# The high part of every fourth weight unit by a casting DMA, in a two-layer encoder trunk on one core

## The chip, the cores and the metric

One core of one Trainium2 chip runs the whole forward pass in one launch. The metric is the device time of that launch in microseconds (us); lower is better. The reference is in float32, and the kernel keeps to its accuracy by splitting every operand of a large product in two.

## The reference

Two post-norm layers over 256 tokens of 2048 channels. The first mixes tokens with bidirectional gated linear attention, the second with a 2-D neighbourhood attention of 16 heads; each is followed by a gated conv feed-forward with 5632 channels in either half. Cut to what matters here:

```python
for i in range(DEPTH):                      # DEPTH = 2
    m = _gla_mixer(x, ...) if i % 2 == 0 else _na_mixer(x, ...)
    x = _layer_norm(DEEPNORM_ALPHA * x + m, ln_mix_g[i], ln_mix_b[i])
    f = _conv_ffn(x, ffn_w_up[i], ffn_conv_w[i], ffn_conv_b[i], ffn_w_down[i])
    x = _layer_norm(DEEPNORM_ALPHA * x + f, ln_ffn_g[i], ln_ffn_b[i])

def _conv_ffn(x, w_up, conv_w, conv_b, w_down):
    h = x @ w_up
    hp = jnp.pad(h, ((0, 0), (1, 1), (0, 0)))
    h = hp[:, :-2] * conv_w[0] + hp[:, 1:-1] * conv_w[1] + hp[:, 2:] * conv_w[2] + conv_b
    a, b = jnp.split(h, 2, axis=-1)
    return (jax.nn.gelu(a, approximate=False) * b) @ w_down
```

In the neighbourhood attention a head computes `softmax(q k * scale + bias)` over its window and multiplies by v.

## The kernel before

All weights are cut into 393 units in the order in which TensorE takes them (`unit_plan`); all but one are of 1 MB, 128 partitions of 2048 float32. A "ws" unit holds 128 output channels for all 2048 input channels and stands still in the array while the tokens stream; an "as" unit holds 512 input channels by 512 output channels and is streamed against the activations.

TensorE multiplies float32r, a rounded float32. So a unit is loaded into a `raw` buffer (three of them, by SyncE's DMA queue, L127) and split: `hi` is the rounded copy, made by ScalarE (L131), and `lo` the rest, made by VectorE (L132), each in four pieces of 512 columns. There are four `hi` and four `lo` buffers (`NS = 4`), so that a unit's `hi` goes into the buffer that TensorE read four units earlier. A product takes three terms: hi by hi, hi by lo and lo by hi (L190).

`pump` writes the splits and loads into the program: when a unit has been used (`finish`), the split of the unit four later is emitted, with a priority lowered by `SPLIT_AFTER = 20`. A tile framework then sets each engine's order by the priorities and adds the waits. Each engine works strictly in that order.

Beside the split VectorE evacuates the products. In the feed-forward's up-projection it joins two halves (L461), waits for GpSimd's multiply of the convolution (L642), adds two taps (L643, L644) and multiplies the gate (L660). In attention it joins q and k, scales and biases the scores into `s` (L724), takes the maximum (L728), and after ScalarE's exponential the reciprocal (L733), and scales `s` (L735), which TensorE then transposes (L742). A head's scores, transposes and last product are put into TensorE's order between the products of the following weights, a fixed number of steps after its k (`later(score, 3, ...)`, `turn` 7, `pv` 9). GpSimd also issues the loads of biases (L701) and LayerNorm parameters (L344).

```python
    def emit_split(src, hi, lo):
        nc.scalar.copy(hi, src)
        nc.vector.tensor_tensor(lo, src, hi.bitcast(F32), ALU.subtract)
```

Of the kernel before, what the change touches and what calls it, by code (L numbers as in the profile page):

```python
# [10 lines left out]
F32 = mybir.dt.float32  # L11
# [6 lines left out]
P = 128  # L18
# [29 lines left out]
def unit_plan():  # L48
    """The 1 MB weight units in the order in which the tensor engine takes them."""
    plan = []  # L50
    for h in range(HG):
        plan += [("ws", "gla_in", h * 2 + c) for c in range(2)]
        plan += [("ws", "gla_in", 8 + h * 2 + c) for c in range(2)]
        if h == 0:
            plan += [("lr",)]
        plan += [("as", "gla_in", 4 + h, u) for u in range(4)]
        plan += [("as", "gla_in", 8 + h, u) for u in range(4)]
    plan += [("as", "gla_out", nb, u) for nb in range(4) for u in range(4)]
    for layer in range(DEPTH):
        if layer == 1:  # L60
            for g in range(4):
                plan += [("as", "na_in", 8 + g, u) for u in range(4)]
                for h in range(4 * g, 4 * g + 4):
                    plan += [("ws", "na_in", h), ("ws", "na_in", 16 + h)]
            plan += [("as", "na_out", nb, u) for nb in range(4) for u in range(4)]
        for c0, n in THIRDS:
            if c0 == 0:
                plan += [("pairs", f"up{layer}", u) for u in range(4)]
            for c in range(c0 + (2 if c0 == 0 else 0), c0 + n):
                plan += [("ws", f"up{layer}", c), ("ws", f"up{layer}", NCT + c)]  # L70
            plan += [("as", f"down{layer}", nb, u)
                     for nb in range(4) for u in range(c0 // 4, (c0 + n) // 4)]
    return plan
# [3 lines left out]
def kernel(  # L77
# [36 lines left out]

    raws, splits = {}, {}
    st = {"load": 0, "split": 0, "done": 0, "next": 0, "tick": 0}

    def pieces(n):
        return [slice(c * 2048 // n, (c + 1) * 2048 // n) for c in range(n)]

    def emit_load(j):
# [12 lines left out]
    def pump():  # L134
        while st["split"] < min(n_units, st["done"] + NS):
# [4 lines left out]
            r = raws.pop(j)  # L140
            hi = hi_p.tile([P, 2048], F32R, tag="hi", name="hi")
            lo = lo_p.tile([P, 2048], F32R, tag="lo", name="lo")
            if plan[j][0] == "lr":
                # three copies of the columns, for the three terms of the gates' product
                src = r[:, :512].rearrange("p (k m) -> p k m", m=32)
                h4 = hi[:, :KC * 96].rearrange("p (k c m) -> p k c m", c=3, m=32)
                l4 = lo[:, :KC * 96].rearrange("p (k c m) -> p k c m", c=3, m=32)
                for c in range(3):
                    emit_split(src, h4[:, :, c], l4[:, :, c])
            else:  # L150
                for sl in pieces(4):
                    with tc.high_priority(offset=-SPLIT_AFTER):
                        emit_split(r[:, sl], hi[:, sl], lo[:, sl])
            splits[j] = (hi, lo)
            st["split"] = j + 1
            if st["load"] < n_units:
# [3 lines left out]
    def take():  # L160
        """The parts of the next unit."""
        pump()
# [10 lines left out]
    def later(fn, delay=1, chain=True):  # L173
        """Emit fn in `delay` ticks: after the item queued before it, or from now on."""
        now = st["tick"]
# [15 lines left out]

# [1 line left out]
    def ws_part(xs, hi, lo, ps, kcs):  # L193
# [15 lines left out]

# [1 line left out]
    def as_mm(xs, k, kc, hi3, lo3, ps, t, start, stop):  # L211
# [4 lines left out]
    def as_block(xs, n, evac, apart=False, settle=False):  # L216
        """n units (4 chunks of K each) for one block of 512 columns."""
        ps = [ps_mm(), ps_mm()]
# [41 lines left out]

# [1 line left out]
    ident = const.tile([P, P], F32, name="ident")  # L262
# [6 lines left out]

# [1 line left out]
    def rsqrt(dst, src, scale, eps, small):  # L271
        """(src * scale + eps) ** -0.5"""
        m = small.tile([P, 1], F32, tag="rs_m", name="rs_m", bufs=2)
# [13 lines left out]
    def ln_mid(pool, xs, t, stats, idx, gb):  # L287
        """LayerNorm between sub-layers: xT for the products, xs for the residual."""
        def head():
# [57 lines left out]
    def residual_out(act_in, first, last, n, idx, begin=None):  # L347
        """Four blocks of columns of a product that ends a sub-layer, and the LayerNorm after it."""
        stats = {}
# [23 lines left out]

# [1 line left out]
    scope = {"stack": ExitStack()}  # L375
# [15 lines left out]

    # the first units and x in pieces of K, so that the products start with the first of them
    n_first = NR
# [32 lines left out]

    # the gates as one product over 98 rows: (lr, weights) as (hi, hi), (lo, hi), (hi, lo), and the bias
    lrT = gla.tile([98, T], F32R, name="lrT")
    nc.gpsimd.memset(lrT[96:98, :].bitcast(F32), 1.0)
    # +1 on the rows with weights' high parts, -1 on those with their low parts; 0 and 1  # L430
    sgn = gla.tile([98, 2], F32, name="sgn")
# [24 lines left out]
    def join(pool, dst, ps):  # L456
        """The sum of the two parts of a weights-stationary product."""
        ps4 = ps.rearrange("p (t h n) -> p t h n", t=2, h=2)
# [4 lines left out]
    def gla_head(h):  # L463
# [17 lines left out]
        def gates(z):  # L481
# [12 lines left out]
            else:  # L494
                nc.vector.tensor_tensor_scan(c_[:, ::-1], smask[:, 512:0:-1], la[:, ::-1], 0.0, ALU.mult, ALU.add)
            # [channel, tile of channels, block of 128, half, token]
            c5 = c_.rearrange("p (c b s n) -> p c b s n", c=2, b=2, s=2)
# [9 lines left out]
        def decay(z):  # L507
# [12 lines left out]
            kx[z] = gla.tile([P, 2, P], F32, tag=f"kx{z}", name="kx")  # L520
            # forward: queries of block 1 over chunk 2, keys of block 0 over chunk 1; backward: the mirror
            qb, kb = (1, 0) if z == 0 else (0, 1)
# [7 lines left out]
        def scores():  # L530
            # main[j, jt, it, i]: backward on the diagonal, the crossing blocks beside it
            main, diag = ps_tp(), ps_tp()
# [88 lines left out]

# [1 line left out]
    def ffn(layer):  # L623
# [23 lines left out]
        for part, (c0, n) in enumerate(THIRDS):  # L647
# [16 lines left out]
            if part == 0:  # L664
                # two pairs with the activations stationary, one token tile after the other
                ht = {}
# [23 lines left out]

# [1 line left out]
    def attention():  # L692
# [81 lines left out]

# [1 line left out]
    for h in range(HG):  # L776
# [23 lines left out]
def lay_out(a):  # L800
    """The inputs as the kernel reads them: orders, repeats and zero padding only."""
    mats = {"gla_in": a["gla_w_in"][0], "gla_out": a["gla_w_out"][0],
# [67 lines left out]
```

## Time and profile before

| | |
|---|---|
| time, median of 2 runs | 2319.48 us (2319.03 to 2319.93) |
| span of the profiled execution, first to last instruction | 2314.5 us |
| TensorE matmul (PE) busy | 2267.8 us |
| VectorE (DVE), ScalarE (ACT), GpSimd (POOL) busy | 1576.1, 1139.4 and 314.9 us |
| DMA traffic | 432.84 MB, mean 187 GB/s |

The profile is of one execution. The page gives its span and no launch-to-end time of its own, so the runs' median is what stands beside it, 5.0 us longer. A view by lines groups instructions by the line of the kernel that issued them; "x" gives their count. In a timeline an instruction's idle time ahead and what ended it stand in square brackets. A busy TensorE counts pipelined matmuls, so it isn't TensorE at its peak. L-numbers are lines of the kernel before.

### The profile page before, as it was taken

The page shows a single profiled execution, that of the slowest core. Times are in us where ns is not written, and L with a number is a line of the kernel's source. Part 1 is how long each engine was busy: PE and PEld are TensorE (multiplying, and loading weights), DVE is VectorE, ACT ScalarE, POOL GpSimd, SP SyncE. Part 2 cuts the span into 40 slices and gives each one's busy share as a digit, 9 for nine tenths or more (in the row PEclk, how much of TensorE's full clock was granted, in tenths as well). Part 3 has the DMA queues.
Part 4 walks back from the last instruction along what each step waited for, and adds up shares of the span by engine and source line. Part 5 has one row for each costly group of instructions (what it writes and reads, how often), then busy time and mean ns, then how long its engine had stood idle before and what let it go on. Part 6 is the DMA issues. An engine that isn't in the chain of part 4 may idle for free. (4 is left out here: it accounts for less than half of the span.)

```text
span 2314.5 us, 31264 instructions
## 1 busy us (share of the span) xinstructions
PE 2267.8 (98%) x11728; PEld 1929.9 (83%) x11728; DVE 1576.1 (68%) x2831; ACT 1139.4 (49%) x2307; POOL 314.9 (14%) x333
## 2 busy tenths in 40 slices
PE   8999999899999999999989999989999999999997
PEld 7888887788888888888778888878888888888886
DVE  7666656877557775676686776668775577656775
ACT  6655544554445553444455555445554455444542
POOL 1100002311001110011230111023110011100111
PEclk9999999999999999999999999999999999999999
DMA  7544463555555555555445544545555555555552
GB/s 275 185 164 182 178 260 140 208 196 187 195 187 182 186 193 196 188 184 191 155 178 187 183 174 177 220 144 210 193 187 194 190 191 182 192 190 185 189 191 91
DMA packets 63879, 432.84 MB, mean 187 GB/s; under 512 B 7344, under 2 KB 7344, under 8 KB 12784
## 3 DMA queue, kind: packets, MB, share of 16 engines
q1 hardware_dynamic: 60336, 415.00, 49.8%
q0 software_dynamic: 3104, 15.32, 1.8%
q8 instruction: 92, 1.51, 0.3%
q10 hardware_dynamic: 288, 0.52, 0.1%
q14 instruction: 59, 0.48, 0.1%
HBM read 428.72 MB, written 2.10 MB: 186 GB/s over the span
## 5 line engine op out<-in xcount | busy, mean ns | idle before, releaser
L132 DVE TENSOR_TENSOR lo<-raw,hi 128x512 fp32r<-128x512 f32 x1571 | 1056.3, 701 | 449.7 <-ACT hi L131 448.5
L190 PE MATMUL ps_mm<-xT,hi 128*128 128x512 f32 x3472 | 1231.9, 399 | 6.6 <-ACT hi L131 5.9
L131 ACT CAST hi<-raw 128x512 fp32r<-128x512 f32 x1571 | 884.7, 619 | 615.4 <-PE ps_mm L190 486.9
L190 PE MATMUL ps_mm<-xT,lo 128*128 128x256 f32 x3472 | 976.2, 281 | 0.0
L190 PEld LDWEIGHTS ps_mm<-xT,hi 128*128 128x128 f32 x3472 | 653.2, 188 | 167.0 <-ACT hi L131 5.9
L190 PEld LDWEIGHTS ps_mm<-xT,lo 128*128 128x128 f32 x3472 | 656.9, 189 | 1.5 <-DVE lo L132 0.9
L190 PE MATMUL ps_mm<-hi,gT 128*128 128x512 f32 x1920 | 595.5, 390 | 0.0
L190 PEld LDWEIGHTS ps_mm<-hi,gT 128*128 128x128 f32 x1920 | 360.4, 188 | 74.9
L190 PE MATMUL ps_mm<-lo,gT 128*128 128x512 f32 x960 | 373.5, 389 | 0.0
L642 POOL TENSOR_SCALAR c<-h,cw,cb 128x256 f32<-128x256 f32 x168 | 149.9, 892 | 1171.6 <-DVE h L461 1171.6
L190 PE MATMUL ps_mm<-hi,xT 128*128 128x512 f32 x896 | 286.5, 394 | 0.0
L190 PEld LDWEIGHTS ps_mm<-lo,gT 128*128 128x128 f32 x960 | 180.3, 188 | 36.8
L190 PEld LDWEIGHTS ps_mm<-hi,xT 128*128 128x128 f32 x896 | 170.3, 190 | 35.5 <-DVE xT L132 0.5
L190 PE MATMUL ps_mm<-lo,xT 128*128 128x512 f32 x448 | 177.2, 395 | 7.6 <-DVE lo L132 7.5
L131 ACT CAST gT<-gg 128x256 fp32r<-128x256 f32 x88 | 35.8, 407 | 230.5 <-DVE gg L660 230.5
L643 DVE SCALAR_TENSOR_TENSOR c<-h,cw,c 128x255 f32<-128x255 f32 x168 | 81.2, 484 | 77.9 <-POOL c L642 77.9
L655 ACT ACTIVATE ge<-c 128x256 f32<-128x256 f32 x88 | 36.8, 418 | 156.5 <-DVE c L644 156.5
L190 PEld LDWEIGHTS ps_mm<-lo,xT 128*128 128x128 f32 x448 | 85.5, 191 | 26.3 <-DVE lo L132 9.4
L644 DVE SCALAR_TENSOR_TENSOR c<-h,cw,c 128x255 f32<-128x255 f32 x168 | 80.2, 477 | 0.0
L460 ACT COPY join_t<-ps_mm 128x256 f32<-128x256 f32 x216 | 78.9, 365 | 0.0
L461 DVE TENSOR_TENSOR h<-ps_mm,join_t 128x256 f32<-128x256 f32 x168 | 70.1, 417 | 0.0
L132 DVE TENSOR_TENSOR gT<-gg,gT 128x256 fp32r<-128x256 f32 x88 | 37.4, 425 | 38.7 <-ACT gT L131 38.7
(131 smaller groups left out, 870.1 us busy)
## 6 DMA issues: line engine op xcount, KB each, us to landing
raw<-in_w_dram SPq DMA_DIRECT2D x388, 1024.0 KB, 4.8
gb<-in_lnp_dram POOLq DMA_DIRECT2D x8, 1024.0 KB, 10.4
raw<-in_w_dram SPq DMA_DIRECT2D x16, 256.0 KB, 5.7
bt<-in_bias_dram POOLq DMA_DIRECT2D x16, 192.0 KB, 2.9
xr<-in_xt_dram SPq DMA_DIRECT2D x8, 256.0 KB, 5.6
x_sb<-in_x_dram POOLq DMA_DIRECT2D x1, 2048.0 KB, 10.3
out_dram<-x_sb SPq DMA_DIRECT2D x6, 256.0 KB, 2.3
gu<-in_gup_dram POOLq DMA_DIRECT2D x4, 196.0 KB, 3.3
```

Of the source, the lines that this page charges most:

```text
L131: nc.scalar.copy(hi, src)
L132: nc.vector.tensor_tensor(lo, src, hi.bitcast(F32), ALU.subtract)
L190: nc.tensor.matmul(o, l, r, start=start, stop=stop)
L460: nc.scalar.copy(tmp, ps4[:, :, 1])
L461: nc.vector.tensor_tensor(dst.rearrange("p (t n) -> p t n", t=2), ps4[:, :, 0], tmp, ALU.add)
L642: nc.gpsimd.tensor_scalar(c, hh, w_[:, 1:2], cb[:, ch:ch + 1], ALU.mult, ALU.add)
L643: nc.vector.scalar_tensor_tensor(c[:, 1:], hh[:, :T - 1], w_[:, 0:1], c[:, 1:], ALU.mult, ALU.add)
L644: nc.vector.scalar_tensor_tensor(c[:, :T - 1], hh[:, 1:], w_[:, 2:3], c[:, :T - 1], ALU.mult, ALU.add)
L655: nc.scalar.activation(ge, c, AF.Gelu)
```

## The change

Every fourth unit after the first six (the condition is in `by_dma`; 97 of the 393 units) gets its `hi` by a DMA that GpSimd issues from the weights in memory straight into the float32r buffer, which rounds on the way. ScalarE's four casts of such a unit are left out. The unit is still loaded into `raw`, and VectorE subtracts as before (now L158; the cast DMA is L164, the unchanged split L136). The DMA of unit j + 1 is emitted right behind the split of unit j. Comments that the change deletes are left out here.

```diff
-    raws, splits = {}, {}
+    raws, splits, cast = {}, {}, {}
...
+    def by_dma(j):
+
+        return j > 2 * NR and j % 4 == 0 and plan[j][0] != "lr"
...
-            hi = hi_p.tile([P, 2048], F32R, tag="hi", name="hi")
+            hi = cast.pop(j) if j in cast else hi_p.tile([P, 2048], F32R, tag="hi", name="hi")
...
                 for sl in pieces(4):
                     with tc.high_priority(offset=-SPLIT_AFTER):
-                        emit_split(r[:, sl], hi[:, sl], lo[:, sl])
+                        if by_dma(j):
+                            nc.vector.tensor_tensor(lo[:, sl], r[:, sl], hi[:, sl].bitcast(F32), ALU.subtract)
+                        else:
+                            emit_split(r[:, sl], hi[:, sl], lo[:, sl])
             splits[j] = (hi, lo)
+            if j + 1 < n_units and by_dma(j + 1):
+                cast[j + 1] = hi_p.tile([P, 2048], F32R, tag="hi", name="hi")
+                nc.gpsimd.dma_start(cast[j + 1], w[slot[j + 1]])
```

VectorE's order in the second head of a group of four in attention, before; `k` is the end of the evacuation of the head's k, the rows from `s` on are its softmax, and numbers tell buffers apart:

```order
L132 TENSOR_TENSOR lo_10562<-raw_10386,hi_10561 128x512 x2
L132 TENSOR_TENSOR k_10440<-qk_10555,k_10440 128x256
L132 TENSOR_TENSOR gT_81<-ps_tp_10587,gT_81 128x2x128
L132 TENSOR_TENSOR lo_10562<-raw_10386,hi_10561 128x512
L724 SCALAR_TENSOR_TENSOR s_10612<-ps_tp_10613,bt_10441 128x256 x2
L728 TENSOR_REDUCE nm_10622<-s_10612 128x2
L132 TENSOR_TENSOR lo_10646<-raw_10437,hi_10645 128x512
L733 RECIPROCAL rc_10627<-sm_10624 128x2
L735 TENSOR_SCALAR s_10612<-s_10612,rc_10627 128x256 x2
```

Here the subtractions of one unit are spread between the evacuations, and one stands within the softmax. The same place in the changed kernel:

```order
L136 TENSOR_TENSOR k_10290<-qk_10407,k_10290 128x256
L136 TENSOR_TENSOR gT_81<-ps_tp_10434,gT_81 128x2x128
L158 TENSOR_TENSOR lo_10413<-raw_10236,hi_10362 128x512 x4
L734 SCALAR_TENSOR_TENSOR s_10459<-ps_tp_10460,bt_10291 128x256 x2
L471 TENSOR_TENSOR qk_10486<-ps_mm_10425,join_t_10487 128x256
L738 TENSOR_REDUCE nm_10469<-s_10459 128x2
L136 TENSOR_TENSOR q_10420<-qk_10486,q_10420 128x256
L136 TENSOR_TENSOR lo_10493<-raw_10287,hi_10492 128x512 x2
L743 RECIPROCAL rc_10474<-sm_10471 128x2
L136 TENSOR_TENSOR lo_10493<-raw_10287,hi_10492 128x512
L745 TENSOR_SCALAR s_10459<-s_10459,rc_10474 128x256 x2
```

All four subtractions of the cast unit now stand together ahead of `s`, and three of the next unit's, with the evacuation of q, within the softmax. It is so in the second and the fourth head of each of the four groups, but that in the fourth no q is evacuated there.

GpSimd's order at the end of an up-projection, before (convolution multiplies only) and then in the changed kernel:

```order
L642 TENSOR_SCALAR c_9117<-h_9113,cw_3446,cb_3448 128x256
L642 TENSOR_SCALAR c_9174<-h_9170,cw_3446,cb_3448 128x256
L642 TENSOR_SCALAR c_9229<-h_9225,cw_3446,cb_3448 128x256
L642 TENSOR_SCALAR c_9286<-h_9282,cw_3446,cb_3448 128x256
L642 TENSOR_SCALAR c_9341<-h_9337,cw_3446,cb_3448 128x256
```

Each multiply waits for VectorE's join of its own unit. In the changed kernel:

```order
L164 DMA hi_9170<-in_w_dram 128x2048
L652 TENSOR_SCALAR c_9211<-h_9207,cw_3398,cb_3400 128x256
L652 TENSOR_SCALAR c_9263<-h_9259,cw_3398,cb_3400 128x256
L652 TENSOR_SCALAR c_9318<-h_9314,cw_3398,cb_3400 128x256
L652 TENSOR_SCALAR c_9375<-h_9371,cw_3398,cb_3400 128x256
L164 DMA hi_9391<-in_w_dram 128x2048
L652 TENSOR_SCALAR c_9432<-h_9428,cw_3398,cb_3400 128x256
```

A casting DMA stands behind every fourth multiply. It waits there until TensorE has ended the unit whose `hi` buffer it writes, and the multiplies behind it wait with it.

## Rows read from the trace of the kernel before

**Rows 1.** The page's busy times: engine, busy us, share of the span, instructions.
```profile
PE 2267.8 (98%) x11728; PEld 1929.9 (83%) x11728; DVE 1576.1 (68%) x2831; ACT 1139.4 (49%) x2307; POOL 314.9 (14%) x333
```

**Rows 2.** Windows: up-projection, down-projection, attention, a LayerNorm; the first line names the columns.
```profile
core 0: us, PE busy (x) PEld busy (x) DVE busy (x) ACT busy (x) POOL busy (x), PEclk, DMA share, GB/s
1680.00:1740.00 60.00, 60.00 (x342) 52.00 (x341) 43.54 (x86) 29.29 (x63) 9.21 (x11) 1.00 0.51 182
2040.00:2100.00 60.00, 60.00 (x267) 49.67 (x266) 30.17 (x49) 24.03 (x44) 0.00 (x0) 1.00 0.55 194
1260.00:1320.00 60.00, 60.00 (x350) 52.62 (x349) 44.46 (x87) 33.40 (x80) 6.46 (x8) 1.00 0.53 186
1140.00:1200.00 60.00, 51.39 (x245) 42.31 (x244) 53.05 (x79) 32.78 (x66) 33.53 (x25) 0.94 0.42 150
```

**Rows 3.** Waits: who waited <- for whom: us in total, times, longest us.
```profile
ACT hi L131 <- PE ps_mm L190: 486.9, 223, 11.4
DVE lo L132 <- ACT hi L131: 448.5, 319, 4.0
...
ACT hi L131 <- DMA raw<-in_w_dram: 20.0, 13, 3.8
...
PE ps_mm L190 <- ACT hi L131: 5.9, 1, 5.9
```

**Rows 4.** Costliest groups, ScalarE's cast: count | busy us, mean ns | idle.
```profile
L131 ACT CAST hi<-raw 128x512 fp32r<-128x512 f32 x1571 | 884.7, 619 | 615.4 <-PE ps_mm L190 486.9
```

**Rows 5.** Line L344, pairs of 1 MB loads, GpSimd's queue; issue ns min/median/max.
```profile
L344 POOL DMA_DIRECT2D gb<-in_lnp_dram x8: 528/559/612, 311.6 to 1577.6; - x8
...
DMA to landing us min/median/max: 5.4/10.4/18.9
```

**Rows 6.** Line L127, the weights' loads on SyncE's queue, likewise.
```profile
L127 SPq DMA_DIRECT2D raw<-in_w_dram x392: 327/328/432, 20.8 to 2266.7; - x196
...
DMA to landing us min/median/max: 4.1/4.8/10.4
```

**Rows 7.** Timeline of VectorE in an up-projection: start us, us, instruction [idle before].
```profile
1700.86 0.69 DVE L132 TENSOR_TENSOR lo<-raw,hi 128x512 fp32r<-128x512 f32 x1 [1.49 <-ACT hi L131]
...
1702.94 0.48 DVE L643 SCALAR_TENSOR_TENSOR c<-h,cw,c 128x255 f32<-128x255 f32 x1 [0.47 <-POOL c L642]
...
1705.83 0.42 DVE L132 TENSOR_TENSOR gT<-gg,gT 128x256 fp32r<-128x256 f32 x1 [0.47 <-ACT gT L131]
1706.51 0.69 DVE L132 TENSOR_TENSOR lo<-raw,hi 128x512 fp32r<-128x512 f32 x1 [0.26 <-ACT hi L131]
...
1708.60 0.48 DVE L643 SCALAR_TENSOR_TENSOR c<-h,cw,c 128x255 f32<-128x255 f32 x1 [0.46 <-POOL c L642]
```

**Rows 8.** Timeline of VectorE in attention, second layer.
```profile
1298.48 1.28 DVE L132 TENSOR_TENSOR lo<-raw,hi 128x512 fp32r<-128x512 f32 x2
1299.69 0.42 DVE L132 TENSOR_TENSOR k<-qk,k 128x256 fp32r<-128x256 f32 x1
...
1302.69 0.76 DVE L724 SCALAR_TENSOR_TENSOR s<-ps_tp,bt 128x256 f32<-128x256 f32 x2 [1.65 <-PE ps_tp L190]
1303.48 0.69 DVE L728 TENSOR_REDUCE nm<-s 128x2 f32<-128x512 f32 x1
...
1305.56 0.17 DVE L733 RECIPROCAL rc<-sm 128x2 f32<-128x2 f32 x1 [0.30 <-ACT s L731]
1305.76 0.61 DVE L735 TENSOR_SCALAR s<-s,rc 128x256 f32<-128x256 f32 x2
1306.29 0.42 DVE L461 TENSOR_TENSOR qk<-ps_mm,join_t 128x256 f32<-128x256 f32 x1
1306.62 0.68 DVE L132 TENSOR_TENSOR lo<-raw,hi 128x512 fp32r<-128x512 f32 x1
```

**Rows 9.** Timeline of ScalarE in the same head.
```profile
1296.89 0.62 ACT L131 CAST hi<-raw 128x512 fp32r<-128x512 f32 x1 [0.70 <-PE ps_mm L190]
```

**Rows 10.** Timeline of TensorE in the same head, the transposes of s.
```profile
1308.07 0.60 PE L742 MATMUL ps_tp<-ident,s 128*128 128x128 f32 x4
```

## The prediction

> **What bounds the kernel now.** I read the busy shares first. TensorE is busy for 2267.8 of the 2314.5 us of the span, and no other engine comes near; ScalarE stands at 49% [rows 1]. Such a share is an average, so the stretches come next. In the conv feed-forward, in its down-projection and in attention TensorE is busy for 60.00 of 60 us; only a stretch with a LayerNorm shows a gap, 51.39 of 60 [rows 2]. The granted clock is 1.00, the 2.4 GHz level, in the first three and 0.94 on average in the last, where TensorE had idled before.
>
> Third, the waits. The idle time that ScalarE's casts of weights cause is large, but it falls on VectorE (448.5 us), and ScalarE itself waits as long for TensorE to release a `hi` buffer (486.9 us). TensorE waited for a cast of weights once, for 5.9 us [rows 3]. So splitting of weights runs ahead of TensorE, and a cheaper split has at most those 5.9 us to win.
>
> **What the change removes.** There are 393 units and 97 of them go to the DMA, so 97 x 4 = 388 casts at 619 ns, 240 us of ScalarE, disappear [rows 4]. ScalarE's time lies beside TensorE's, and I cost this at nothing. It can give back 0 to 6 us.
>
> **What it adds on the queues.** 97 more transfers of 1 MB are issued by GpSimd, at 559 ns each [rows 5]: 54 us of an engine that is busy 14% of the span [rows 1]. The weights' own loads keep the DMA share at 0.51 to 0.55 [rows 2]; a quarter more of such traffic makes it about 0.65. A weight load lands after 4.1 to 10.4 us, median 4.8 [rows 6]. It is issued when VectorE has finished the unit three before it, and is wanted three units later; with units 5.65 us apart [rows 7] and some 5.5 us of splitting ahead of the issue that leaves 3 x 5.65 - 5.5 = 11.4 us. Even the slowest landing of before fits, so I cost the loads' delay at nothing.
>
> **What it adds on the way to TensorE.** VectorE still makes `lo`, 4 x 0.60 us a unit in issue distance (two start at 1298.48 and the next instruction at 1299.69, so that each takes 0.69 us of which 0.09 lie beside its successor [rows 8]). But the first of the four now waits for the whole transfer. The buffer that the transfer writes is the one that TensorE reads four units earlier, so the transfer is issued when that unit ends, the moment at which ScalarE's cast started before. Call T the time from there to landing. ScalarE delivered its first quarter after some 0.65 us; the DMA delivers everything after T. What is queued behind the waiting subtraction on VectorE are the evacuations of other products, and who waits for those decides the price.
>
> No row shows a casting DMA. The nearest is a plain 1 MB transfer of the same queue: 5.4 us at the least, 10.4 us in the median, where two are issued together and the second stands in line [rows 5]. So T is between 5.4 and 10.4 us if the cast itself costs nothing or up to as much as a second transfer. I take 6.5 us: the lone plain one, and about 1 us for the weight load that it shares the engines with, since it is nearest to that row.
>
> The Trainium skill weighs in on both sides. In "DMA: Bandwidth & Descriptors", section on the anatomy of one SWDGE DMA, a transfer costs 2.0 us and its bytes at 436 GB/s; by that estimate T would be 4.4 us, under the 5.4 us of the row, and the total below would be 2322 us. The same page, section "Issuing engines are not separate DMA queues", says that transfers from all issuers interleave on the same engines; by that a cast that meets a whole load would take 5.4 us and the 2.9 us that a load keeps the engines (0.51 of 60 us over the 10.4 loads of a window of 182 GB/s), 8.3 us, and the total would be 2362 us. The rows stand between the two.
>
> **Attention, the term that counts.** In 8 of the 16 heads the order puts the four subtractions of a cast unit straight ahead of the softmax's `s`. From the rows of one head, which all heads repeat [rows 8 to 10]: TensorE ends the unit of its k (ScalarE's cast follows it at 1296.89) and takes the transposes of `s` at 1308.07, 11.2 us later. VectorE finishes `s` at 1306.37, so 1.7 us early. In the changed order, after T, VectorE does four subtractions (2.4 us) and then its chain, in which three subtractions and the evacuation of q stand where one subtraction stood: 0.76 + 0.33 + 0.60 + 0.33 + 3 x 0.60 + 0.2 + 0.61 = 4.6 us. With 0.1 us of hand-over, TensorE is held if T is over 11.2 - 2.4 - 4.6 - 0.1 = 4.1 us, and by the excess. At 6.5 us: 8 x 2.4 = 19 us. At 5.4 us 10 us; at 10.4 us 50 us.
>
> **Conv feed-forward.** 42 casts fall in its up-projections. There VectorE has slack: two units, 11.3 us, have waits of 1.49, 0.47, 0.47, 0.26 and 0.46 us in them [rows 7]. One after the other the work goes on, only later, and TensorE is three units (17 us) ahead of need. The limit is GpSimd's queue, where the next cast stands behind the convolution's multiply of the unit before. After the subtractions VectorE needs two units of 4.8 us (4.1 busy, and 0.7 waiting for GpSimd and ScalarE) and 2.1 us until that multiply is done, so at T + 2.4 + 9.6 + 2.1, and the next transfer is due at 4 x 5.65 = 22.6 us. Up to T = 8.5 us nothing is lost; beyond it each of the 42 loses the excess. At 6.5 us the cost is 0, hidden by VectorE's slack.
>
> **Down-projections and the rest.** In these stretches VectorE is busy for 30.17 of 60 us and GpSimd idle [rows 2]: 38 casts, nothing lost. There are some nine other tight places: the four starts of a group of heads, a chain of gated linear attention, four LayerNorms, three of them on TensorE's path. If all had attention's margin they would add 9 x 2.4 = 22 us, if none, 0. I take 5 us, since the LayerNorms' DMAs were issued earlier and ScalarE is less laden there.
>
> **Sum.** 0 - 0 + 19 + 0 + 5 = 24 us. The span of the profiled execution is 2314.5 us; the runs' median, 2319.48 us, lies 5.0 us above it, launch and end, which the change doesn't touch. 2319.5 + 24 = 2343.5, so 2344 us, 1.0% longer. A measurement tells about 2% (46 us) from no change, so this counts as the same.
>
> **The rivals.**
> - *The casting transfer is slow.* The datapath works on each element, and T passes 8.4 us. Place: attention's `s` and, from 8.5 us on, GpSimd's queue in the feed-forward. At T = 10.4 us: 8 x 6.3 = 50, 42 x 1.9 = 80, and 15 elsewhere, 145 us in all: 2464 us. It is slower by over 2% from T = 8.4 us on (34 and 12 us). For it: no casting transfer in the trace, and the median of 10.4 us. Against: the first of two plain ones lands in 5.4 us. 0.36.
> - *It gives the little that ScalarE held.* T is near 4 us, or the chains have more room than I read, and the 5.9 us go: 2314 us. For it: all that ScalarE did is taken off. Against: TensorE is busy 60.00 of 60 us. 0.06, and 0.01 for more than 2%, which would need 46 of the 47 us in which TensorE idles at all.
> - *The weight loads come late.* They share the engines with the casts, and pass the 11.4 us of room. At 12.4 us on each of 97 occasions, 97 us: 2416 us. Against: ScalarE waited for a load only 13 times, 20.0 us [rows 3]. 0.03.
> - *The change does less than it says*: transfers wait on GpSimd behind other work, so that T is long by waiting. GpSimd has nothing to do for 86% of the span, and this is within the first rival's numbers.
>
> **How the numbers follow.** The forecast has 0.54, with its own range from T = 5.4 us and nothing elsewhere (2329) to T = 8.4 us (2366). The small gain has 0.06. So within 2%: 0.60; slower by over 2%: 0.36 + 0.03 = 0.39; faster: 0.01. The range reaches down to 2318, which leaves out most of the small gain, and up to 2470 for T = 10.4 us, with about 0.15 beyond.
>
> **What would show it right or wrong.** Landing of the new DMAs: 6 to 7 us would confirm T. Attention's windows should lose about 2.4 us in each of 8 heads, as TensorE waiting at the transposes of `s` for VectorE, and VectorE should wait for the DMA in front of `lo` 97 times. The feed-forward should stay at 60.00 of 60. If TensorE waits there, T is over 8.5 us. If ScalarE waits for `raw` much more than 20 us, the third rival holds. If TensorE waits nowhere new, I have misread the margins.

## The result and the profile after

The changed kernel took 2346.24 us (median of 2 runs, 2345.95 to 2346.53) against 2319.48 us: a ratio of 1.0119, with a 95% interval of 1.0099 to 1.0138. That is 26.8 us more by the medians. The spans of the two profiled executions, 2344.0 and 2314.5 us, differ by 29.5 us, and it is this difference that the traces can explain.

The page of the changed kernel, its busy times, the software queue (packets, MB, share of the 16 DMA engines' time), the groups that answer to [rows 4], and the two kinds of 1 MB transfers (KB each, median us from issue to landing):

```profile
PE 2276.8 (97%) x11728; PEld 1933.2 (82%) x11728; DVE 1563.6 (67%) x2831; ACT 927.8 (40%) x1919; POOL 355.3 (15%) x430
...
q0 software_dynamic: 17072, 117.04, 13.7%
...
L135 ACT CAST hi<-raw 128x512 fp32r<-128x512 f32 x1183 | 666.4, 618 | 638.2 <-PE ps_mm L200 589.6
...
L158 DVE TENSOR_TENSOR lo<-raw,hi 128x512 fp32r<-128x512 f32 x388 | 257.3, 714 | 308.5 <-DMA hi<-in_w_dram 283.8
...
L164 POOL DMA_DIRECT2D hi<-in_w_dram x97 | 55.2, 569 | 847.6 <-PE ps_mm L200 421.8
...
raw<-in_w_dram SPq DMA_DIRECT2D x388, 1024.0 KB, 4.8
hi<-in_w_dram POOLq DMA_DIRECT2D x97, 1024.0 KB, 5.3
```

The 388 casts are gone from ScalarE (1139.4 us busy before, 927.8 now), and GpSimd issues 97 transfers in 55.2 us. A casting transfer lands 5.3 us after its issue, half a microsecond more than a plain weight load. TensorE is busy 9.0 us longer with the same 11728 instructions, in part at the lower clock; the rest of the 29.5 us is idle time.

The stretches of [rows 2] in the changed kernel, and one near the start (columns as there):

```profile
60.00:120.00 60.00, 56.76 (x289) 47.74 (x288) 38.87 (x72) 31.04 (x59) 7.58 (x11) 0.97 0.60 214
1140.00:1200.00 60.00, 51.04 (x232) 41.24 (x231) 49.94 (x72) 24.94 (x51) 34.68 (x27) 0.94 0.49 178
1260.00:1320.00 60.00, 58.22 (x323) 50.40 (x323) 37.34 (x71) 25.28 (x57) 5.78 (x8) 0.97 0.58 209
1680.00:1740.00 60.00, 60.00 (x341) 52.03 (x340) 40.43 (x80) 23.22 (x51) 9.72 (x13) 1.00 0.62 226
2040.00:2100.00 60.00, 60.00 (x270) 49.75 (x269) 35.47 (x61) 20.74 (x40) 3.17 (x5) 1.00 0.70 255
```

Up- and down-projection still hold TensorE at 60.00 of 60 us with more DMA traffic. The attention stretch lost 1.8 us, and its mean granted clock fell from 1.00 to 0.97.

The waits of the changed kernel (who waited <- for whom: us in total, times, longest), answering to [rows 3]:

```profile
PE ps_tp L752 <- DVE s L745: 15.2, 8, 2.8
PE ps_mm L200 <- DVE lo L158: 6.7, 3, 2.5
PE ps_mm L200 <- ACT hi L135: 6.2, 1, 6.2
PE ps_tp L200 <- ACT sh L135: 3.2, 1, 3.2
...
PE ps_tp L200 <- ACT k L135: 1.1, 1, 1.1
PE ps_tp L200 <- DVE k L136: 0.7, 1, 0.7
...
DVE lo L158 <- DMA hi<-in_w_dram: 283.8, 84, 6.7
...
ACT hi L135 <- DMA raw<-in_w_dram: 16.1, 11, 3.5
```

New on TensorE are the 15.2 us at the transposes of `s`, eight times, 3.2 us in gated linear attention, and 1.8 us at the products of q and k in one head of the first group in attention. ScalarE waits for weight loads 11 times and 16.1 us, against 13 times and 20.0 us before with a third more casts to make, so those aren't late. VectorE waits for a cast 84 times, where the prediction had 97.

A second look cuts the span at the LayerNorms, by the two BATCH_NORM_AGGREGATE rows of VectorE that each of the four leaves. For the first LayerNorm of the changed kernel they are:

```profile
391.04 0.26 DVE L292 BATCH_NORM_AGGREGATE ln_mv<-ln_st 128x2 f32<-128x24 f32 x1
...
412.48 0.26 DVE L292 BATCH_NORM_AGGREGATE ln_mv<-ln_st 128x2 f32<-128x24 f32 x1
```

Gated linear attention and its output projection thus take 391.04 us from the start of the span. Each stretch runs from the second such row of a LayerNorm to the first of the next one. In us, for all profiled executions, the experiments of the next section included:

| | start to 1st LayerNorm | 1st feed-forward | attention and output projection | 2nd feed-forward | after the last row |
|---|---|---|---|---|---|
| before | 385.13 | 734.47 | 380.93 | 734.45 | 10.8 |
| changed | 391.04 | 734.52 | 404.41 | 734.50 | 10.8 |
| e1_none_in_attention | 390.92 | 734.43 | 386.32 | 736.00 | 11.0 |
| e2_only_in_attention | 385.69 | 734.41 | 396.69 | 734.46 | 10.8 |
| e4_none_in_both | 385.68 | 736.08 | 387.74 | 734.47 | 15.9 |
| e8_inside_feed_forward | 385.00 | 734.46 | 382.04 | 736.05 | 14.7 |
| e9_at_layernorms | 385.52 | 734.45 | 386.59 | 734.49 | 10.9 |
| e3_four_pieces | 394.29 | 734.96 | 404.87 | 734.97 | 15.6 |
| e10_load_behind | 391.85 | 734.45 | 393.63 | 734.49 | 10.9 |
| e11_load_held | 395.17 | 734.47 | 389.96 | 736.02 | 10.8 |
| e6_cast_twice | 401.81 | 762.80 | 443.75 | 753.92 | 10.8 |
| e7_phase3 | 402.69 | 738.69 | 394.18 | 737.38 | 10.8 |

The table settles where the 29.5 us are: 23.5 between the second and the third LayerNorm, 5.9 before the first, 0.1 in 1469 us of feed-forward. Each row is one execution, though. Up to the first LayerNorm the changed kernel, e1, e10 and e11 run the same instructions in the same order on every engine, and they take 390.92 to 395.17 us; in the second feed-forward, where that is so again, they take 734.49 to 736.02 us. A difference of 1 to 2 us between two rows, and of up to 4 us before the first LayerNorm, can thus come about with no change of the kernel.

### The profile page after: what moved, and what is told of

It reads as the page before. It is cut to its first block, busy times and chain, and to the rows that moved or that the text cites. A ratio compares the mean times of both kernels' runs of the same rounds, so it can differ in the third digit from the quotient of the medians.

```text
span 2344.0 us, 30950 instructions
## 1 busy us (share of the span) xinstructions
PE 2276.8 (97%) x11728; PEld 1933.2 (82%) x11728; DVE 1563.6 (67%) x2831; ACT 927.8 (40%) x1919; POOL 355.3 (15%) x430
## 5 line engine op out<-in xcount | busy, mean ns | idle before, releaser
L135 ACT CAST hi<-raw 128x512 fp32r<-128x512 f32 x1183 | 666.4, 618 | 638.2 <-PE ps_mm L200 589.6
L136 DVE TENSOR_TENSOR lo<-raw,hi 128x512 fp32r<-128x512 f32 x1183 | 780.5, 695 | 134.6 <-ACT hi L135 130.5
L158 DVE TENSOR_TENSOR lo<-raw,hi 128x512 fp32r<-128x512 f32 x388 | 257.3, 714 | 308.5 <-DMA hi<-in_w_dram 283.8
L652 POOL TENSOR_SCALAR c<-h,cw,cb 128x256 f32<-128x256 f32 x168 | 136.1, 810 | 718.6 <-DVE h L471 718.6
L164 POOL DMA_DIRECT2D hi<-in_w_dram x97 | 55.2, 569 | 847.6 <-PE ps_mm L200 421.8
L653 DVE SCALAR_TENSOR_TENSOR c<-h,cw,c 128x255 f32<-128x255 f32 x168 | 81.3, 484 | 92.0 <-POOL c L652 91.9
## 6 DMA issues: line engine op xcount, KB each, us to landing
gb<-in_lnp_dram POOLq DMA_DIRECT2D x8, 1024.0 KB, 10.2
```

What stands on the lines that cost most here:

```text
L158: nc.vector.tensor_tensor(lo[:, sl], r[:, sl], hi[:, sl].bitcast(F32), ALU.subtract)
L164: nc.gpsimd.dma_start(cast[j + 1], w[slot[j + 1]])
L652: nc.gpsimd.tensor_scalar(c, hh, w_[:, 1:2], cb[:, ch:ch + 1], ALU.mult, ALU.add)
L653: nc.vector.scalar_tensor_tensor(c[:, 1:], hh[:, :T - 1], w_[:, 0:1], c[:, 1:], ALU.mult, ALU.add)
```

## The experiments

My theory after this: a cast costs nothing by its traffic or its issue, and something only where VectorE, waiting for it, has a short chain behind it that TensorE needs. The rival: every cast costs a little, by traffic or by the issuing engine.

**Leaving casts out by stage.** Five kernels narrow the rule that picks the units; the last two replace it:

```
e1: ... and plan[j][1] != "na_in"                        (85 casts)
e4: ... and plan[j][1] not in ("na_in", "gla_in")        (74 casts)
e2: ... and plan[j][1] == "na_in"                        (12 casts)
e8: j % 4 == 0 and (76 <= j <= 188 or j >= 272)          (60 casts)
e9: j in (64, 68, 72, 192, 196, 200, 244, 248, 252, 256, 260, 264, 268)
```

Expected of the first, without casts in the attention's input units:

> Attention's 12 casts go back to ScalarE; 85 casts stay. Theory (VectorE stands in front of a landing cast while TensorE waits for the softmax): the 16.9 us that TensorE idles in the windows of attention, two of the three new half-clock stretches (2 x 1.7 us) and the slower restarts (8 x 0.45 us) go, 24 us: 2322 us, and no wait of the transposes of s for VectorE is left. Rival (the extra 100 MB of traffic slows everything): 85 of 97 casts remain, so 2346 - 3 = 2343 us.

It took 2328.27 us, against 2316.96 us of the kernel before in the same series (ratio 1.0048, interval 1.0032 to 1.0064). Of the 23.5 us of attention 18.1 are gone (404.41 to 386.32 us), but 11.3 us in all remain, more than I expected, and one wait of 2.4 us at the transposes of `s` stays, in the last head.

> The 12 casts of attention alone. Theory: 2319.5 + 24 = 2343 us, with the same eight waits at the transposes of s (some 15 us). Rival (traffic): 12 of 97 casts, 2319.5 + 3 = 2323 us.

It took 2332.50 us, ratio 1.0067 (1.0052 to 1.0082): 15.5 us for 12 casts, less than the 24 I expected, and six waits in place of eight. The whole loss sits in the attention's stretch (396.69 against 380.93 us) and its waits of the transposes are

```profile
PE ps_tp L752 <- DVE s L745: 10.4, 6, 2.4
```

> No casts in attention and none in gated linear attention's input projections; 74 casts stay. Theory: the wait of 3.2 us for sh and its half-clock stretch go as well, and the rest of the casts costs nothing and gains nothing: 2319 us, within 2 us of before. Rival (traffic): 2346 - 23/97 x 27 = 2340 us. Rival (ScalarE's relief is worth something): under 2315 us.

It took 2328.56 us, ratio 1.0048 (1.0033 to 1.0063), and so missed all three numbers; against e1's 2328.27 us nothing was won. The table tells in part why: gated linear attention did get back 5.2 us (390.92 to 385.68), as the theory has it. But this execution had 1.6 us more than the kernel before in the first feed-forward and 5 us more after its last LayerNorm row. In the first place TensorE waited 3.00 us for `lo` behind the LayerNorm (2.27 us in the kernel before) and then ran 3.4 us longer at the granted clock of 0.5, the 1.2 GHz level. In the second, GpSimd's DRAIN, an instruction at the end of the program, takes 10.7 us in place of 4.7, and the other engines' last instructions come behind it. The two views of the program's last line, of the kernel before and of e4 (count, ns min/median/max, first and last start):

```profile
L866 POOLq DRAIN  x3: 46/102/4656, 2308.1 to 2314.2; - x3
L876 POOLq DRAIN  x3: 46/93/10701, 2317.1 to 2328.3; - x3
```

> Casting transfers only for units well inside the two feed-forwards (60 of 97: units 76 to 188 and 272 to 392 in steps of four, none near a LayerNorm, none in the gated linear attention, the attention or their output projections). Theory (the feed-forward hides the whole wait; what the runs without casts in the attention still lost, some 11 us, comes from the few casts that stand beside a LayerNorm or reach into the last head): the same as before, 2314 to 2321 us, TensorE without idle in every feed-forward stretch, half-clock stretches as before. Rival (the extra traffic, GpSimd's issuing or the clock take a little at every cast, 11 us over some 80 casts): 60/80 of it, about 2325 us.

It took 2323.73 us against 2319.02 us, ratio 1.0018 (1.0009 to 1.0028). The number lies nearer the rival's, yet the table doesn't place the loss where the casts are. The first feed-forward, with 29 casts, takes 734.46 us against 734.47. (The second, with 31, has the 1.6 us below.) The excess of this execution is 1.6 us of one more stretch at 1.2 GHz behind the third LayerNorm, where TensorE had waited 2.79 us for a unit that isn't cast by a transfer, 1.1 us in the attention, which has no casts here, and 3.9 us after the last LayerNorm row, where GpSimd's DRAIN takes 9.6 us. So within the feed-forward's stretches no cost of the casts shows. Why the DRAIN takes longer is open: it takes 3.9 us in the changed kernel with its 97 casts. So the runs don't show whether the 4.7 us by the medians are a cost of the casts.

> The complement: 13 casting transfers, only for the units beside the three inner LayerNorms (64, 68, 72, 192, 196, 200, 260, 264, 268) and from the last head through the attention's output projection (244, 248, 252, 256). Theory: nearly all of the remaining loss is here although only 13 of 97 units are cast by a transfer: 2325 to 2331 us, with one wait of the transposes of s of about 2.3 us in the last head and one or two more half-clock stretches of 3.4 us than before. Rival (every cast costs a little): 13/80 of 11 us, about 2319 us.

It took 2323.33 us, ratio 1.0025 (1.0013 to 1.0037), between the two numbers. Nearly its whole excess is in the attention's stretch, 386.59 against 380.93 us, where TensorE waits 4.1 us at the transposes of `s` in 3 heads: two of the 13 units (200 and 244) still belong to the attention's input, and the first of the output projection stand in the last head. The LayerNorms themselves lose nothing. In all the runs above their two rows lie 21.4, 17.0 and 21.4 us apart, as before.

The parts nearly add up. The casts of the attention's input units cost 15.8 us in its stretch (e2), the others 5.4 us there (e1), 21.2 of the 23.5 us of all together. Gated linear attention's own cost most of the 5.9 us there: e1 keeps 5.8 of them, and e4 is left with 0.6.

**Four transfers instead of one.** If VectorE waits for a whole transfer, pieces should let it start sooner.

```
-                nc.gpsimd.dma_start(cast[j + 1], w[slot[j + 1]])
+                for sl in pieces(4):
+                    nc.gpsimd.dma_start(cast[j + 1][:, sl], w[slot[j + 1]][:, sl])
```

> Each cast in four DMAs of 512 columns, so that VectorE's first subtraction waits for a quarter only. Theory: the first quarter lands after some 3.5 us, the last near 6 us, subtractions run beside the landings, and the heads' waits of 15.2 us shrink to about 3 us: 2333 us. Rival (what counts is the last byte, and four issues of 0.57 us on GpSimd and smaller rows make it later): 2346 us or more.

It took 2351.65 us, ratio 1.0143 (1.0127 to 1.0160); the rival held. The pieces land 4.7 us after their issue in the median, and they are issued one behind the other at 557 ns each, which brings GpSimd to 519.5 us. By the trace the first subtraction does start sooner, 3.7 us after the first issue in the median (5.7 us in the changed kernel), but the last quarter lands 8.8 us after it (5.3 us). The waits at the transposes of `s` fell to 12.3 us only, and the attention's stretch is no shorter, 404.87 us. The scheduler also changed VectorE's order in this kernel, so the 5.4 us between it and the changed kernel aren't put down to the pieces alone.

**What makes a cast take longer in a head.** In the timelines of the changed kernel one head has the cast ahead of the weight load on the queues, and the next has it behind. The first, then the second:

```profile
1218.58 0.55 POOL L164 DMA_DIRECT2D hi<-in_w_dram  x1 [1.49 <-PE ps_mm L200]
1219.21 0.33 SPq L131 DMA_DIRECT2D raw<-in_w_dram  x1
1224.02 0.69 DVE L158 TENSOR_TENSOR lo<-raw,hi 128x512 fp32r<-128x512 f32 x1 [2.46 <-DMA hi<-in_w_dram]
1230.72 0.30 PE L752 MATMUL ps_tp<-ident,s 128*128 128x128 f32 x1 [0.17 <-DVE s L745]
...
1244.74 0.33 SPq L131 DMA_DIRECT2D raw<-in_w_dram  x1
1245.29 0.55 POOL L164 DMA_DIRECT2D hi<-in_w_dram  x1 [2.07 <-PE ps_mm L200]
1252.87 2.50 DVE L158 TENSOR_TENSOR lo<-raw,hi 128x512 fp32r<-128x512 f32 x4 [4.82 <-DMA hi<-in_w_dram]
1255.29 0.75 DVE L734 SCALAR_TENSOR_TENSOR s<-ps_tp,bt 128x256 f32<-128x256 f32 x2
...
1259.06 0.61 DVE L745 TENSOR_SCALAR s<-s,rc 128x256 f32<-128x256 f32 x2
...
1259.56 1.07 PE L752 MATMUL ps_tp<-ident,s 128*128 128x128 f32 x4 [2.56 <-DVE s L745]
```

From issue to the first subtraction it is 5.4 us in the first head and 7.6 us in the second; TensorE waits 0.17 and 2.56 us. In either the slack, the time that a cast may take before TensorE has to wait, is about 5 us (5.4 - 0.2 and 7.6 - 2.6). The same difference is 5.0 to 5.3 us in all eight heads. To make sure that it is the load, I tried to issue it behind the cast.

```
-                nc.sync.dma_start(r[:, sl], w[slot[j]][:, sl])
+                (nc.gpsimd if by_dma(j - NR + 1) and plan[j - NR + 1][1] == "na_in" else nc.sync).dma_start(r[:, sl], w[slot[j]][:, sl])
```

> As the changed kernel, but in the attention the weight load that SyncE issued about 0.5 us ahead of each casting transfer is issued by GpSimd behind the cast instead; the order on VectorE moves with it in most heads (the two adds of the bias and the row maximum of the head now stand ahead of the four low parts of the cast unit). Theory (a head's cast took 7.0 us from its issue to the first low part only because the load's packets went first, 5.3 us without, and what a head loses is this time less the slack of its softmax): from issue to first low part 5.1 to 5.7 us in all heads, the waits of the transposes of s down from 15.2 us to under 3, 2327 to 2332 us. Rival (the 7.0 us are the attention's other traffic, not the load): still about 7 us, and 2338 to 2346 us.

It took 2334.99 us, ratio 1.0073 (1.0057 to 1.0089), between the two, but not by the way I meant. The scheduler put the load ahead of the cast on GpSimd's queue in all heads but the first. The first took 5.2 us; the others took about 7.1 us, as in 1246.33 to 1253.44. The waits of the transposes fell to 5.4 us with casts that were no faster, and what differs ahead of them is that the first half of the softmax now stood ahead of the subtractions on VectorE. So VectorE's order is worth some 10 us of waits here, and the load's part stays open. The next kernel therefore holds the load back by a dependence and leaves every other engine's order as it was:

```
+            if by_dma(j - NR + 1) and plan[j - NR + 1][1] == "na_in": nc.gpsimd.tensor_scalar(r[:, :1], cast[j - NR + 1][:, :1].bitcast(F32), 1.0, None, ALU.mult)
```

> As the changed kernel, but in the attention a one-column operation of GpSimd reads the cast's buffer and writes the weight buffer first, so that the weight load that went out about 0.5 us ahead of the cast waits until the cast has landed; the orders on VectorE, ScalarE, TensorE and SyncE are those of the changed kernel. Theory (a head's cast takes 7.0 us from its issue to the first low part because the load's packets go first; without them 5.3, beside a slack of about 5.0): 5.0 to 5.7 us in all heads, the waits of the transposes of s down from 15.2 us to under 4, the stretch from the second to the third LayerNorm down from 404.4 us by 11 to 15, 2331 to 2336 us. Rival (other traffic makes the 7.0 us): still about 7 us and 2344 to 2347 us.

It took 2335.03 us, ratio 1.0065 (1.0050 to 1.0080), as the theory had it, with waits a little over its 4 us. The same head as above, in the timelines of this kernel, and its waits at the transposes:

```profile
1249.10 0.55 POOL L165 DMA_DIRECT2D hi<-in_w_dram  x1 [2.02 <-PE ps_mm L201]
1254.26 0.69 DVE L159 TENSOR_TENSOR lo<-raw,hi 128x512 fp32r<-128x512 f32 x1 [2.65 <-DMA hi<-in_w_dram]
1254.39 0.64 POOL L130 TENSOR_SCALAR raw<-hi 128x1 f32<-128x1 f32 x1 [4.74 <-DMA hi<-in_w_dram]
1255.06 5.87 SPq L132 DMA_DIRECT2D raw<-in_w_dram  x3
1260.95 0.72 PE L753 MATMUL ps_tp<-ident,s 128*128 128x128 f32 x4 [0.39 <-DVE s L746]
...
PE ps_tp L753 <- DVE s L746: 4.5, 8, 2.2
```

The cast takes 5.2 us with the load behind it, TensorE waits 0.39 us in place of 2.56, and the attention's stretch is 14.5 us shorter (404.41 to 389.96 us). In the seven heads with no load ahead the cast takes 5.0 to 5.2 us and TensorE waits 0.2 to 0.6 us. A weight load that goes out 0.5 to 1.4 us ahead thus delays the cast by some 2 us, and this makes up more than half of what attention loses. (The 2.2 us in the waits' last column are the last head, whose load is not held.) How far ahead it goes counts: three casts of the changed kernel, at 1274.26, 1352.89 and 1431.46, followed their load by 2.5 us and took 5.1 us to the first subtraction. Why so isn't shown.

**A slower cast.** The transfer is issued twice into the same buffer:

```
                 nc.gpsimd.dma_start(cast[j + 1], w[slot[j + 1]])
+                nc.gpsimd.dma_start(cast[j + 1], w[slot[j + 1]])
```

> As the changed kernel, but each casting transfer is issued twice into the same buffer, the second behind the first, so that the high part is complete only some 10.6 us after its issue (5.3 us twice; about 12.3 in the heads of the attention). Theory of the prediction (each stage hides the wait up to its own limit: about 5.0 us in a head, 8.5 us in the feed-forward, and pays us for us above it): heads 8 x 7.3 = 58 us, gated linear attention some 30, feed-forward 64 x 2.1 = 134, on top of about 2329: about 2550 us, with idle TensorE in every feed-forward stretch of 60 us. Rival A (the feed-forward's limit is far higher than 8.5, only the attentions pay): about 2420 us and feed-forward stretches still at 60.00 of 60. Rival B (every us of every cast reaches the end): 2344 + 97 x 5.3 = about 2860 us.

It took 2421.69 us (2406.53 to 2436.00), ratio 1.0443 (1.0388 to 1.0497): rival A's number. By the table the profiled execution, the longest of them, loses 62.8 us in attention, 28.3 and 19.5 us in the feed-forwards, where the theory had 134 and rival A nothing. The 62.8 us are near the theory's 58, but by another way. The scheduler changed VectorE's order here too: the softmax of a head now stands ahead of the cast unit's subtractions, no transpose of `s` waits, and the eight waits are at the next row, the eviction of `pt`:

```profile
PE ps_tp L201 <- DVE pt L136: 25.7, 8, 5.8
```

So this run tests neither the slack of 5.0 us nor the order of the changed kernel. The second transfer goes out only behind the landing of the first, 5.2 us or more after its issue, and a pair takes 10.3 to 16.9 us to the first subtraction. Three windows of this kernel, an up-projection, an attention and another up-projection:

```profile
840.00:900.00 60.00, 56.44 (x289) 47.45 (x289) 35.49 (x71) 23.00 (x50) 9.80 (x14) 0.97 0.72 263
1260.00:1320.00 60.00, 54.95 (x283) 46.50 (x282) 37.42 (x69) 23.66 (x55) 7.03 (x10) 0.94 0.61 226
1740.00:1800.00 60.00, 60.00 (x348) 52.47 (x347) 40.24 (x80) 26.14 (x58) 11.28 (x17) 1.00 0.78 281
```

In the last, with TensorE full, a cast runs from 1740.35 to VectorE's first subtraction at 1753.32:

```profile
1740.35 0.58 POOL L164 DMA_DIRECT2D hi<-in_w_dram  x1
...
1753.32 1.29 DVE L158 TENSOR_TENSOR lo<-raw,hi 128x512 fp32r<-128x512 f32 x2 [3.30 <-DMA hi<-in_w_dram]
```

So 13 us are hidden here. The limit in the feed-forward, in this kernel's order, is far above the 8.5 us that I had worked out. Whether it is the same in all parts isn't shown: two casts of the first of the three windows took 13.8 and 14.9 us to the first subtraction (from 837.86 and 862.63), so one limit of some 13 us would do for both.

**Other units.** The last kernel casts as many units, one place earlier (`j % 4 == 3`).

> The same number of casting transfers, but for units 4n+3 instead of 4n: in the attention the four low parts of a cast unit then stand right behind the scaling of s on VectorE instead of ahead of the whole softmax. Theory (what costs time is only a wait that stands ahead of a head's softmax in VectorE's order): the transposes of s wait under 2 us in all, the stretch from the second to the third LayerNorm 381 to 390 us (404.4 in the changed kernel), 2322 to 2334 us. Rival (each of the attention's casts costs about 1.5 us wherever it stands, through the queue or the engine that waits): 2341 to 2349 us; the next row on VectorE, the eviction of pt, would then hold TensorE.

It took 2356.91 us, ratio 1.0159 (1.0142 to 1.0176): slower than the rival's range. What was expected came in attention, where no transpose of `s` waits any more and the stretch is 10.2 us shorter than in the changed kernel (394.18 us, above the 390 expected). But the wait only moved to what now stands behind the subtractions, and to other stages. These are the waits of this kernel:

```profile
PE ps_tp L309 <- DVE x_sb L303: 28.8, 4, 10.7
...
PE ps_tp L200 <- DVE v L136: 6.4, 3, 2.9
...
PE ps_tp L200 <- DVE pt L136: 4.1, 6, 1.4
```

The LayerNorms' transposes now wait 28.8 us in all (17.0 in the changed kernel) and up to 10.7 us in one place, the start of the span lasts 11.7 us longer, and `pt` and `v` hold TensorE. VectorE's order differs from that of the changed kernel in all stretches, so this run doesn't price a single place. My expectation was too narrow: it named the softmax alone, where any chain that TensorE needs soon will do.

## Why the prediction was right, and where it was not

The time, 2344 us, was 2 us off, and the direction and the main place were right: TensorE waits at the transposes of `s` in the eight heads that were named. That the number came so close is luck in part, step by step:

- **ScalarE, nothing gained**: right. The one wait of TensorE for a cast of weights stayed, 6.2 us against 5.9.
- **Queues, nothing lost**: right. The DMA share rose to 0.62 in the up-projection and 0.70 in the down-projection, about the 0.65 forecast, and the rival of late weight loads falls: 16.1 us of ScalarE's waits for them in place of 20.0.
- **T = 6.5 us**: right only as a mean of two cases, and by the prediction's own sign, landings of 6 to 7 us, not confirmed: the median of the 97 casts is 5.3 us. In the heads of attention a cast with no load just ahead takes 5.0 to 5.4 us, at or under the 5.4 us of the row that I took as the lower bound [rows 5], and one behind a weight load 6.9 to 7.9 us. Seven of the eight heads that wait have a load just ahead; I had added 1 us for it, and it is some 2 us. The rival of a slow transfer falls with this: it needed 8.4 us and more, and the casts exceed plain loads by half a microsecond in the median.
- **Attention, 8 x 2.4 = 19 us**: the step that was mis-sized is the slack, 4.1 us. It is 5.0. From the issue to the transposes there is room for 11.8 us (1297.89 to 1311.43, less a wait of 1.78 us), where I took 11.2 from ScalarE's next cast, and the chain behind the subtractions takes 4.3 us with the hand-over, not 4.7. The two errors nearly cancel: seven heads wait 1.8 to 2.8 us and the first 0.2, where I had 2.4 in each; 15.2 us in all in place of 19.
- **What a wait costs besides itself** was in no term. The attention's stretch lost 23.5 us, 8.3 more than its waits at `s`. By the two windows below TensorE idles 17.3 us more there, 1.8 of them at the products of q and k, and is busy 6.2 us longer with the same 2000 instructions. Part of that is the clock: behind the two longest of the eight waits, 2.56 us before 1259.56 and 2.84 us before 1498.17, the granted clock fell to 0.5 for 3.4 us, some 1.7 us lost each time. The 2.8 us of busy time that are left the runs don't place.

The head from whose rows the room and the chain are taken, in the changed kernel's timelines:

```profile
1297.89 0.55 POOL L164 DMA_DIRECT2D hi<-in_w_dram  x1 [2.04 <-PE ps_mm L200]
1304.74 2.50 DVE L158 TENSOR_TENSOR lo<-raw,hi 128x512 fp32r<-128x512 f32 x4 [4.07 <-DMA hi<-in_w_dram]
1311.43 0.30 PE L752 MATMUL ps_tp<-ident,s 128*128 128x128 f32 x1 [1.78 <-DVE s L745]
```

The attention's stretch before and in the changed kernel, columns as in [rows 2]:

```profile
1158.07:1539.00 380.93, 375.01 (x2000) 322.56 (x2001) 264.74 (x478) 191.13 (x423) 47.62 (x48) 0.99 0.52 186
1164.02:1568.43 404.41, 381.23 (x2000) 324.56 (x2001) 258.81 (x478) 161.40 (x361) 55.07 (x64) 0.98 0.59 217
```

The first of the two waits in windows of 2 us (PE busy, PEclk, DMA share, GB/s), with TensorE idle in the first and at 1.2 GHz right after it:

```profile
1258.00:1260.00 2.00, 0.44 (x3) 0.94 0.97 409
1260.00:1262.00 2.00, 2.00 (x7) 0.50 0.85 242
1262.00:1264.00 2.00, 2.00 (x10) 0.71 0.72 295
```

- **Nine other places, 5 us**: near the 5.9 us measured before the first LayerNorm. But they are one chain of gated linear attention (3.2 us of wait, and one more such stretch of the clock between 74 and 80 us); the LayerNorms lost nothing, and the starts of a group of heads only the 1.8 us at the products of q and k in the first group. That 5 us came near 5.9 is luck.
- **Feed-forward, nothing lost**: right, 0.1 us in 1469. The limit of 8.5 us behind it was too low, as far as the doubled cast with its other order tells: it still hides at 13 us in one part. Which term of my chain overlaps with the next the runs don't say.

The Trainium skill's two rules stood on either side. "DMA: Bandwidth & Descriptors", section on the anatomy of one SWDGE DMA, gave an estimate of 4.4 us for a lone transfer; the trace has 5.0 to 5.4 us in attention, and the total by it, 2322 us, was too low. By the section "Issuing engines are not separate DMA queues" of the same page a cast meets the load's packets on the same engines. The trace agrees, 5.4 against 6.9 to 7.9 us, and e11 bears it out by holding the load back, though the cast didn't lose the whole 2.9 us of a load that I had worked out with it and the total of 2362 us was too high. The rows that I had put between the two were 5.4 and 10.4 us, and the second lies outside.

The spans differ by 29.5 us and the medians by 26.8 probably because the profiled execution of the kernel before was a short one. An execution's own time lies 2.0 us above its span in the changed kernel and 1.7 in e1, where I had taken the whole 5.0 us between span and median for launch and end.

## What to carry to other kernels

A transfer that replaces piecewise work of an engine makes the engine behind it wait for the whole of it, and the price is set by what stands next in that engine's order, not by how busy anything is. Work out the slack of each such chain against the transfer's time together with the one that goes out just ahead of it; with 5 us of slack a transfer of 5.0 to 5.4 us cost 0.2 to 0.6 us, and the same transfer behind another about 2 us each time. Where the bottleneck engine is already full, freeing 212 us of another gives nothing.

## What was unexpected of the hardware

- The cast itself costs next to nothing: 1 MB converted on its way lands in 5.3 us from its issue, in a run in which plain loads of the same size take 4.8 us.
- Four transfers of 256 KB issued in a row by GpSimd land 4.7 us after their issue each, in the median, and the last of them 8.8 us after the first issue, where the whole transfer lands after 5.3 us.
- In three of the profiled executions (e3, e4, e8) the span runs on for 14.7 to 15.9 us behind the last LayerNorm row in place of 11, although the last work of the engines lies as close to that row as in the others. What fills the time is GpSimd's DRAIN at the end of the program: 9.6 to 10.7 us in these three and 2.9 to 5.7 us in the others, before and changed kernel included. What it waits for the runs leave open.
- Which waits bring a stretch at 1.2 GHz: one followed those of 2.56 and 2.84 us in attention, and none the five of 1.78 to 2.12 us in the same kernel. Yet in e2 one followed a wait of 1.85 us and none a later one of 2.36 us, so the wait's length alone doesn't tell.
